# Feed-forward input by seven block products instead of eight, in three groups of two units

## The chip, the cores and the metric

The kernel runs on one core of a Trainium2 chip. The metric is the device time of one execution in microseconds (us), shorter being better. A core has five engines with a queue of instructions each: TensorE (PE, matmuls; its weight loads are shown apart as PEld), VectorE (DVE), ScalarE (ACT), GpSimd (POOL) and SyncE (SP, which here issues the transfers from memory). A difference of about 0.2% (1.25 us) is what a measurement of this kernel can tell from no change.

## What is computed

One layer of a decoder with 256 tokens and 1024 features: two mixers side by side, a cross-attention on 256 memory tokens, then a feed-forward block and a last normalisation. The change touches the feed-forward alone:

```python
hn = rmsnorm(h, norm_ffn_g[l])
gu = hn @ w_ffn_in[l]                       # 1024 -> 2 x 2816
h = h + (jax.nn.silu(gu[..., :FFN_HIDDEN]) * gu[..., FFN_HIDDEN:]) @ w_ffn_out[l]
return rmsnorm(h, final_norm_g)
```

Everything is float32. The kernel multiplies in a reduced format (`fp32r`) and keeps the precision by splitting every operand into a high and a low half and adding three products: high by high, high by low, low by high (`mm3t`, lines 237 to 240).

## The kernel before, in words

**Units.** All weights are read once, in units of 128 x 2048 numbers (1 MB), in the order that `plan` writes out (line 44). In the feed-forward, unit `("I", j, kh)` holds the rows `kh` (512 of 1024 features) of 256 gate columns and the matching 256 linear columns, laid side by side as 4 x 512 columns; unit `("O", j)` holds 256 rows of the output weights. There are 11 groups j: 22 input units and 11 output units, in the order I, I, O of the group before.

**Making a unit ready.** `prep` (line 169) lets SP fetch the unit into one of two `raw` buffers, ACT copies it into the high half (`hi`, line 194, two pieces of 1024 columns), and the low half `lo = raw - hi` (line 198) is shared: in each piece DVE takes 576 columns and POOL 448. There are three buffers each for `hi` and `lo`. `nxt` (line 205) makes units ready two ahead of the one in use.

**The cross-attention's output and the turn of h2.** The loop at line 1071 multiplies `wo` for two halves of tokens (t) and two halves of columns (c). `add_h` (line 915) adds the result to the residual H on DVE and sums its squares on ACT. `turn_h2` (line 1059) transposes one quarter of H on PE, DVE multiplies it by the norm's gain (`h2g`), ACT makes its high half `h2h` and POOL its low half `h2l`. Three quarters are turned inside that loop, the last one behind the first product of the feed-forward (line 1134). H is turned without the norm's factor; the factor (`rstd2`) comes in later, in `gate`, as a scale on each token.

**The feed-forward.** `ffn_in` (line 1104) adds one product into a PSUM bank `psi`: 128 tokens by 512 columns over 512 features, which is 4 x 3 matmuls of 512 columns. So a unit has two products (t = 0, 1), 24 matmuls. After the second unit of a group `gate` (line 1086) forms silu(gate) x linear with ACT and DVE. `turn_hid` (line 1094) transposes the 128 x 256 result on PE, ACT and DVE split it; it stands behind the next group's first unit. `ffn_out` (line 1119) multiplies with the output unit, 24 matmuls into four PSUM banks `acc` that are kept to the end.

**What sets the order.** The order on PE is that of the program (line 1252). On the other engines a planner places the instructions; a buffer with several users is waited for by semaphores. Each engine then takes its queue in order.

Of the kernel before, what the change touches and what calls it, by code (L numbers as in the profile page):

```python
# [10 lines left out]
F32 = mybir.dt.float32  # L11
F32R = mybir.dt.float32r
I32 = mybir.dt.int32
AF = mybir.ActivationFunctionType
# [53 lines left out]


ORDER = plan()  # L70


def lay(ws):
# [39 lines left out]
def bc(ap, n, axis):  # L113
    shape = list(ap.shape)
    shape.insert(axis, n)
    return ap.unsqueeze(axis).to_broadcast(shape)


def build(tc, A, out):
    nc = tc.nc  # L120
    V, SC, G, PE, SY = nc.vector, nc.scalar, nc.gpsimd, nc.tensor, nc.sync
    with ExitStack() as ctx:
# [28 lines left out]
        def bank(name, shape=(128, 512)):  # L151
            return sm.tile(list(shape), F32, name=name, tag="sm")
# [762 lines left out]
        def add_h(t, c, ps, scale, ssq):  # L915
            d = H[:, t, c * 512:(c + 1) * 512]
            if scale is None:
                V.tensor_tensor(d, ps, d, op=ALU.add)
            else:
                V.scalar_tensor_tensor(d, ps, scale, d, op0=ALU.mult, op1=ALU.add)  # L920
            j = t2b("hjunk")
            SC.activation(j, d, AF.Square, accum_out=ssq[:, t, c:c + 1])
# [129 lines left out]
        gfin = big("B4", "gfin", (128, 1024))  # L1052
        SY.dma_start(gfin, A["gfin"].to_broadcast([128, 1024]))
        H2 = big("P2", "H2", (128, 2, 8, 256), F32R)
        h2h, h2l = H2[:, 0], H2[:, 1]
        def wo_part(ps, t, c, kh):
            t_part(ps, wo[2 * c + kh], (oxh, oxl), t, kh)

        def turn_h2(t, c):
            ks, ts = slice(4 * c, 4 * c + 4), slice(t * 128, (t + 1) * 128)  # L1060
            bk = bank("h2T", (128, 4, 128))
            for j in range(4):
                k = 4 * c + j
                PE.transpose(bk[:, j], H[:, t, k * 128:(k + 1) * 128], ident)
            g = t2("h2g", (128, 4, 128))
            V.tensor_tensor(g, bk, bc(gv[:, V_FFN + 4 * c:V_FFN + 4 * c + 4], 128, 2), op=ALU.mult)
            SC.activation(h2h[:, ks, ts], g, AF.Copy)
            G.tensor_tensor(h2l[:, ks, ts], g, h2h[:, ks, ts].bitcast(F32), op=ALU.subtract)

        todo = None  # L1070
        for t in range(2):
            for c in range(2):
                ps = mm.tile([128, 512], F32, name="pso", tag="mm")
                wo_part(ps, t, c, 0)
                if todo:
                    turn_h2(*todo)
                wo_part(ps, t, c, 1)
                add_h(t, c, ps, None, ssq2)
                todo = (t, c)


        ring = ("B7", "B14", "B10", "B11", "B12", "B6")
        X2 = (h2h, h2l)
        hid, acc, two, psi, hm = {}, {}, {}, {}, {}

        def gate(o, t):
            r, ps = two["r"][:, t:t + 1], psi.pop((o, t))
            g = t2("fg", (128, 256))
            SC.activation(g, ps[:, 0:256], AF.Silu, scale=r)  # L1089
            u = t2b("fu", (128, 256))  # L1090
            V.scalar_tensor_tensor(u, ps[:, 256:512], r, g, op0=ALU.mult, op1=ALU.mult)  # L1091
            hm[o, t] = u

        def turn_hid(o):
            bk = mm.tile([128, 2, 256], F32, name="hidT", tag="mm")
            for t in range(2):
                u = hm.pop((o, t))
                for j in range(2):
                    PE.transpose(bk[:, j, t * 128:(t + 1) * 128], u[:, j * 128:(j + 1) * 128], ident)
            hd = big(ring[o % 6], "hid", (128, 2, 2, 256), F32R)  # L1100
            split(bk, hd[:, 0], hd[:, 1])
            hid[o] = hd

        def ffn_in(o, kh, t, w):
            if kh == 0:
                psi[o, t] = mm.tile([128, 512], F32, name="psi", tag="mm")
            t_part(psi[o, t], w, X2, t, kh)

        def out_part(o, w, t, c, home=None, u=0, v=512):
            if home is None and (t, c) not in acc:  # L1110
# [8 lines left out]
        def ffn_out(o):  # L1119
            w = by_k(nxt(), 2)  # L1120
            for t in range(2):
                for c in range(2):
                    out_part(o, w, t, c)

        for u in ORDER[at[0]:-2]:
            if u[0] == "O":
                ffn_out(u[1])
                continue
            _, o, kh = u
            w = by_k(nxt(), 4)  # L1130
            for t in range(2):
                ffn_in(o, kh, t, w)
                if (o, kh, t) == (0, 0, 0):
                    turn_h2(1, 1)
                    two["r"] = rstd2(ssq2, "h2")
                if kh == 1:
                    gate(o, t)
            if kh == 0 and o:
                turn_hid(o - 1)

        n = NF // 2 - 1
        wa = by_k(nxt(), 2)
        wb = by_k(nxt(), 2)
        out_part(n - 1, wa, 0, 0)
        turn_hid(n)
        out_part(n - 1, wa, 0, 1)
# [8 lines left out]


        ssq3 = cp.tile([128, 5], F32, name="ssq3")
        hg3 = {i: big(ring[j], "hg3", (128, 512)) for j, i in enumerate(((0, 0), (0, 1), (1, 0)))}  # L1160
# [95 lines left out]
```

## Time and profile before

| | us |
|---|---|
| median of 3 runs | 625.4 (624.79 to 625.51) |
| the profiled execution | 625.08 |
| its span (first to last instruction) | 623.1 |
| PE busy in the span | 615.1 |
| feed-forward, from its first matmul to its last | 431.12 to 616.63 |

The profile is one execution. Rows of the timeline give the start in us from the span's start, the duration in us, the engine, the line, the operation, `out<-in` by the program's names, the shape, and in brackets the idle time just before with what ended it. Rows of busy time in a stretch give PE, PEld, DVE, ACT and POOL in us (with the count of instructions), the granted PE clock as a share of full speed, the DMA share and GB/s. A PE record of a matmul covers its way through the array, so records of neighbours overlap. In groups, `xN` is the count; in the list of transfers the last number is the median time from issue to landing.

### The profile page before, as it was taken

What the parts mean: (1) busy time and instruction counts of PE and PEld (TensorE: products, weight loads), DVE (VectorE), ACT (ScalarE), POOL (GpSimd) and SP (SyncE); (2) the same over time, 40 slices, a digit from 0 to 9 for tenths busy, and PEclk for the clock granted to TensorE, in tenths of its full rate; (3) what the DMA queues carried; (4) which work ended last, traced back from release to release, by engine and by line L of the source; (5) the groups of instructions that cost most, each with busy time, mean ns of one, the idle gap of its engine ahead of it and who ended that gap; (6) DMA issues with size and microseconds to landing.
All of it is one profiled execution on the core that took longest, in us unless ns stands there. A gap on an engine that the chain in (4) does not pass through costs nothing.

```text
span 623.1 us, 8546 instructions
## 1 busy us (share of the span) xinstructions
PE 615.1 (99%) x3153; PEld 513.7 (82%) x3153; DVE 395.6 (63%) x691; ACT 334.1 (54%) x550; POOL 371.5 (60%) x296
## 2 busy tenths in 40 slices
PE   8999999999999999999999999999999999999995
PEld 7888888888877877778888888888888888888884
DVE  7589888979776875748846456754444444444433
ACT  7785554234376866727547556644543344434432
POOL 3888744556544564356857876656655665566553
PEclk9999999999999999999999999999999999999999
DMA  8754553334433333545454544453354455455511
GB/s 346 288 197 149 203 202 136 136 135 147 191 137 135 136 136 136 203 174 191 145 213 189 187 176 178 143 196 135 136 180 175 187 202 184 177 184 198 204 68 68
DMA packets 16890, 107.53 MB, mean 173 GB/s; under 512 B 2000, under 2 KB 2640, under 8 KB 4560
## 3 DMA queue, kind: packets, MB, share of 16 engines
q1 hardware_dynamic: 16128, 106.14, 46.9%
q10 hardware_dynamic: 720, 0.84, 0.4%
q8 instruction: 25, 0.41, 0.3%
q14 instruction: 17, 0.14, 0.1%
HBM read 105.92 MB, written 1.05 MB: 172 GB/s over the span
## 4 chain that ended last, share of the span: by engine, by line
PE 98%; DVE 0%; POOL 0%; issue 0%; POOLq 0%; DVEq 0%
PE pst L238 13%; PE pst L240 13%; PE pst L239 13%; PE psf L259 7%; PE psi L238 6%; PE psi L240 6%; PE psi L239 6%; PE psf L260 4%; PE acc L240 3%; PE acc L238 3%; PE acc L239 3%; PE lp L613 2%; PE psg L514 1%; PE pso L238 1%; PE pso L240 1%; PE pso L239 1%
## 5 line engine op out<-in xcount | busy, mean ns | idle before, releaser
L198 POOL TENSOR_TENSOR lo<-raw,hi 128x448 fp32r<-128x448 f32 x172 | 272.0, 1597 | 181.4 <-ACT hi L194 178.4
L194 ACT ACTIVATE hi<-raw 128x1024 fp32r<-128x1024 f32 (+1 forms) x194 | 196.2, 1037 | 161.1 <-PE pst L240 58.2
L198 DVE TENSOR_TENSOR lo<-raw,hi 128x576 fp32r<-128x576 f32 (+2 forms) x194 | 197.8, 1024 | 127.9 <-ACT hi L194 126.1
L238 PE MATMUL pst<-hi,XX 128*128 128x512 f32 x224 | 90.4, 404 | 0.0
L240 PE MATMUL pst<-hi,XX 128*128 128x512 f32 x224 | 87.4, 390 | 0.0
L239 PE MATMUL pst<-lo,XX 128*128 128x512 f32 x224 | 87.3, 390 | 0.0
L238 PE MATMUL psi<-hi,H 128*128 128x512 f32 x176 | 69.6, 395 | 0.0
L240 PE MATMUL psi<-hi,H 128*128 128x512 f32 x176 | 68.7, 390 | 0.0
L239 PE MATMUL psi<-lo,H 128*128 128x512 f32 x176 | 68.5, 389 | 0.0
L240 PEld LDWEIGHTS pst<-hi,XX 128*128 128x128 f32 x224 | 42.0, 188 | 9.0
L238 PEld LDWEIGHTS pst<-hi,XX 128*128 128x128 f32 x224 | 42.1, 188 | 8.8 <-issue 0.7
L239 PEld LDWEIGHTS pst<-lo,XX 128*128 128x128 f32 x224 | 42.1, 188 | 7.9
L240 PEld LDWEIGHTS psi<-hi,H 128*128 128x128 f32 x176 | 33.0, 188 | 7.1
L239 PEld LDWEIGHTS psi<-lo,H 128*128 128x128 f32 x176 | 33.1, 188 | 6.6
L238 PEld LDWEIGHTS psi<-hi,H 128*128 128x128 f32 x176 | 33.1, 188 | 6.5
L238 PE MATMUL acc<-hi,hid 128*128 128x512 f32 x86 | 33.6, 390 | 0.0
L240 PE MATMUL acc<-hi,hid 128*128 128x512 f32 x86 | 33.5, 389 | 0.0
L239 PE MATMUL acc<-lo,hid 128*128 128x512 f32 x86 | 33.5, 389 | 0.0
L1091 DVE SCALAR_TENSOR_TENSOR fu<-psi,r_h,fg 128x256 f32<-128x256 f32 x22 | 10.6, 483 | 25.1 <-ACT fg L1089 25.1
L1089 ACT ACTIVATE fg<-psi,r_h 128x256 f32<-128x256 f32 x22 | 10.4, 475 | 29.1 <-PE psi L240 29.1
L259 PE MATMUL psf<-H,hi 128*128 128x512 f32 x64 | 22.8, 400 | 0.0
L259 PE MATMUL psf<-XX,hi 128*128 128x512 f32 x64 | 22.6, 396 | 0.0
(336 smaller groups left out, 1199.4 us busy)
## 6 DMA issues: line engine op xcount, KB each, us to landing
raw<-w SPq DMA_DIRECT2D x94, 1024.0 KB, 4.8
raw<-w SPq DMA_DIRECT2D x4, 512.0 KB, 6.5
raw<-w SPq DMA_DIRECT2D x4, 256.0 KB, 4.0
H<-xtok SPq DMA_DIRECT2D x1, 1024.0 KB, 9.6
mraw<-mT SPq DMA_DIRECT2D x1, 1024.0 KB, 4.9
xraw<-xT SPq DMA_DIRECT2D x1, 512.0 KB, 6.5
gfin<-gfin SPq DMA_DIRECT2D x1, 512.0 KB, 3.7
out<-H SPq DMA_DIRECT2D x2, 256.0 KB, 2.0
```

The costliest lines, as they stand in the source:

```text
L194: SC.activation(hi[:, a], raw[:, a], AF.Copy)
L198: eng.tensor_tensor(lo[:, b], raw[:, b], hi[:, b].bitcast(F32), op=ALU.subtract)
L238: PE.matmul(ps, xh, h, start=first, stop=False)
L239: PE.matmul(ps, xh, l, start=False, stop=False)
L240: PE.matmul(ps, xl, h, start=False, stop=last)
L259: PE.matmul(ps, w[0][:, k, a], X2[:, :, k], start=k == 0, stop=False)
L260: PE.matmul(ps[:, 0], w[1][:, k, a], X2[:, 0, k], start=False, stop=k == 7)
L514: PE.matmul(pss[c][t], z[:, k, t * 128:(t + 1) * 128], ws[c][0][:, k], start=z is Xh and k == 0, stop=False)
L613: PE.matmul(ps[:, j], KS[:, a0 + j], QQ[:, a0 + j], start=True, stop=True)
L1089: SC.activation(g, ps[:, 0:256], AF.Silu, scale=r)
L1091: V.scalar_tensor_tensor(u, ps[:, 256:512], r, g, op0=ALU.mult, op1=ALU.mult)
```

## The change

The groups 2 and 3, 5 and 6, 8 and 9 are joined into three **double groups**. A double group has four input units: two halves of features by two groups. With the two halves of tokens this is a product of 2 x 2 by 2 x 2 blocks, which takes eight products of 12 matmuls. The change forms it from seven (P1 to P7), each a product of a sum of token blocks by a sum of weight blocks, with sums of the results. The groups 0, 1, 4, 7 and 10 stay as they were, with two products a unit.

- The list `FFN_PLAN` has 42 entries: 10 plain input units, 21 products, 11 output units. Its order is I0 I0 I1 I1, then P1 P2 O0 P6 P7 P5 O1 P3 P4 (entries 4 to 12), I4 I4 (13, 14), P1 P2 O2 P6 P7 O3 P5 O4 P3 P4 (15 to 24), I7 I7, P1 P2 O5 P6 P7 O6 P5 O7 P3 P4 (27 to 36), I10 I10, O8 O9 O10.
- The four chunks of a double group are fetched together (`load_blocks`, at the entries in `LOADS`) into four buffers of their own. DVE forms the sums of chunks in place (`both`, two pieces of 1024 columns): one at the load, one each ahead of P6, P5 and P4.
- Each of the 42 entries is split by `halve`: ACT in one piece of 2048 columns, DVE 1152 columns, POOL 896 (the first two entries still in two pieces). Every fourth entry uses a new buffer `px`, which lies where the cross-attention's output `ox` was, so four entries can be split at a time; they are prepared three ahead (`prep_u`).
- The sums of token blocks are made once (`token_sums`): four additions on DVE, four pairs of high and low half on ACT and POOL.
- Products are added up in PSUM where they can be; three times a double group ACT copies a partial sum away (`keep`) and DVE adds it to another bank (`whole`).
- The norm's factor is now applied to H ahead of the turn (`rstd_h2`). The first tokens are turned in the last part of the `wo` loop; then the first four units are multiplied for the first tokens, then the second tokens are turned, then the same four units are multiplied for the second tokens.
- The inner units are turned at the entries in `TURNS`, later than before relative to their gate.

```diff
+SEVEN = ("P1", "P2", "P6", "P7", "P5", "P3", "P4")
...
+LOADS = {0: (2,), 10: (5,), 22: (8,)}
+TURNS = {4: (0,), 8: (1,), 15: (2,), 18: (3,), 20: (4,), 27: (5,), 30: (6,), 32: (7,), 38: (8, 9)}
...
+        px = big("P1", "px", (128, 4096), F32R)
...
+        def halve(raw, n):
+            if n % 4 == 3:
+                hi, lo = px[:, 0:2048], px[:, 2048:4096]
+            else:
+                hi = wh.tile([128, 2048], F32R, name="hi", tag="hi")
+                lo = wl.tile([128, 2048], F32R, name="lo", tag="lo")
+            pieces = 2 if n < 2 else 1
+            w = 2048 // pieces
+            for c in range(pieces):
+                a = slice(c * w, (c + 1) * w)
+                SC.activation(hi[:, a], raw[:, a], AF.Copy)
+                cut = (c + 1) * w - POOL_COLS // pieces
+                V.tensor_tensor(lo[:, c * w:cut], raw[:, c * w:cut], hi[:, c * w:cut].bitcast(F32), op=ALU.subtract)
+                G.tensor_tensor(lo[:, cut:a.stop], raw[:, cut:a.stop], hi[:, cut:a.stop].bitcast(F32),
+                                op=ALU.subtract)
+            return hi, lo
...
+        def both(out, x, y, op):
+            for i in range(2):
+                a = slice(1024 * i, 1024 * i + 1024)
+                V.tensor_tensor(out[:, a], x[:, a], y[:, a], op=op)
+
+        def load_blocks(q):
+            blk.clear()
+            for key, tag, c in (("22", "B12", (q + 1, 1)), ("12", "B6", (q + 1, 0)),
+                                ("11", "B10", (q, 0)), ("21", "B11", (q, 1))):
+                blk[key] = big(tag, "b" + key, (128, 2048))
+                SY.dma_start(blk[key], A["w"][where[("I",) + c]])
...
+                both(blk["12"], blk["22"], blk["12"], ALU.subtract)
+
+        def block(name):
+            if name == "P6":
+                both(blk["11"], blk["12"], blk["11"], ALU.add)
+            elif name == "P5":
+                both(blk["12"], blk["22"], blk["11"], ALU.subtract)
+            elif name == "P4":
+                both(blk["21"], blk["21"], blk["11"], ALU.subtract)
+            return blk[{"P1": "11", "P2": "21", "P6": "11", "P7": "12", "P5": "12", "P3": "22", "P4": "21"}[name]]
...
+        def rstd_h2(t):
+            V.tensor_scalar(v2[:, t:t + 1], ssq2[:, 2 * t:2 * t + 1], ssq2[:, 2 * t + 1:2 * t + 2], EPS,
+                            op0=ALU.add, op1=ALU.add)
+            G.tensor_tensor(r2[:, t:t + 1], v2[:, t:t + 1], nhalf[:, :1], op=ALU.pow)
+            hn = []
+            for c in range(2):
+                n = t2("hn")
+                SC.activation(n, H[:, t, c * 512:(c + 1) * 512], AF.Copy, scale=r2[:, t:t + 1])
+                hn.append(n)
+            return hn
...
+        def keep(key, ps, home):
+            SC.activation(home, ps, AF.Copy)
+            kept[key] = home
+
+        def whole(q, t, ps, key):
+            c = t2("fc")
+            V.tensor_tensor(c, ps, kept.pop(key), op=ALU.add)
+            psi[q, t] = c
+            gate(q, t)
+
+        def ffn_product(n):
+            _, q, name = units[n]
+            w = by_k(pair[n], 4)
+            key = {"P1": "A", "P6": "A", "P5": "A", "P3": "A", "P2": "B", "P7": "F", "P4": "F"}[name]
...
+            product(ps, name, w, first)
+            if name == "P1":
+                keep("1", ps, t2("f1"))
+            elif name == "P2":
+                whole(q, 0, ps, "1")
+            elif name == "P6":
+                keep("2", ps, gf[:, 1024:1536])
+            elif name == "P5":
+                keep("4", ps, gf[:, 1536:2048])
+                whole(q + 1, 1, bank_of["F"], "4")
+            elif name == "P3":
+                psi[q + 1, 0] = ps
+                gate(q + 1, 0)
+            elif name == "P4":
+                whole(q, 1, ps, "2")
...
+        prep_u(3)
+        for n in range(4):
+            ffn_in(n, 0)
+        turn_h2(1, hn1)
+        for n in range(4):
+            for q in LOADS.get(n, ()):
+                load_blocks(q)
+            ffn_in(n, 1)
+            if n == 0:
+                token_sums()
+            prep_u(n + 4)
+        for n in range(4, len(units) - 2):
+            for q in LOADS.get(n, ()):
+                load_blocks(q)
+            prep_u(n + 3)
+            for o in TURNS.get(n, ()):
+                turn_hid(o)
...
```

More of the change, by code (lines that the diff above doesn't have):

```diff
@@ L1055, in build @@
         h2h, h2l = H2[:, 0], H2[:, 1]
+        where = {u: i for i, u in enumerate(ORDER)}
+        px = big("P1", "px", (128, 4096), F32R)
+        made_u, pair, blk = [0], {}, {}
+        def halve(raw, n):
[14 more added lines that the diff above has]
+            return hi, lo
@@ new lines, in block, with prep_u @@
+        def block(name):
[6 more added lines that the diff above has]
+            return blk[{"P1": "11", "P2": "21", "P6": "11", "P7": "12", "P5": "12", "P3": "22", "P4": "21"}[name]]
+        units = FFN_PLAN
+        def prep_u(upto):
+            while made_u[0] <= min(upto, len(units) - 1):
+                n = made_u[0]
+                made_u[0] += 1
+                u = units[n]
+                if u[0] == "P":
+                    raw = block(u[2])
+                else:
+                    raw = wr.tile([128, 2048], F32, name="raw", tag="raw")
+                    SY.dma_start(raw, A["w"][where[u]])
+                pair[n] = halve(raw, n)
@@ new lines, in tokens, with product @@
+        def tokens(name):
+            if name in ("P1", "P2", "P4"):
+                t, kh = {"P1": (0, 0), "P2": (0, 1), "P4": (1, 1)}[name]
+                return [[z[:, 4 * kh + k, t * 128:(t + 1) * 128] for k in range(4)] for z in X2]
+            i = {"P5": 0, "P6": 1, "P7": 2, "P3": 3}[name]
+            return [[SS[:, z, i, k] for k in range(4)] for z in range(2)]
+        def product(ps, name, w, first):
+            xh, xl = tokens(name)
+            for k in range(4):
+                for i, (x, z) in enumerate(((xh, w[0]), (xh, w[1]), (xl, w[0]))):
+                    PE.matmul(ps, x[k], z[:, k], start=first and k == 0 and i == 0, stop=k == 3 and i == 2,
+                              skip_group_check=not first)
@@ L1121, in ffn_out @@
+        def ffn_out(n):
+            w = by_k(pair[n], 2)
             for t in range(2):
                 for c in range(2):
[L1123 to L1139, printed above, removed]
+                    out_part(units[n][1], w, t, c)
@@ L1143, in build @@
         n = NF // 2 - 1
-        wa = by_k(nxt(), 2)
-        wb = by_k(nxt(), 2)
+        wa, wb = (by_k(pair[len(units) - 2 + i], 2) for i in range(2))
         out_part(n - 1, wa, 0, 0)
```

130 lines of the change are left out of this document (96 added, 34 removed).

## The prediction

> **What bounds the kernel now.** I read the page's busy times first, then the chain that ended last, then the busy times of the feed-forward stretch alone.
>
> ```profile
> span 623.1 us, 8546 instructions
> ...
> PE 615.1 (99%) x3153; PEld 513.7 (82%) x3153; DVE 395.6 (63%) x691; ACT 334.1 (54%) x550; POOL 371.5 (60%) x296
> ```
> ```profile
> PE 98%; DVE 0%; POOL 0%; issue 0%; POOLq 0%; DVEq 0%
> ```
> ```profile
> 431.12:616.63 185.51, 185.51 (x847) 153.59 (x845) 83.43 (x103) 80.29 (x105) 107.80 (x68) 1.00 0.45 165
> ```
>
> The last row (PE, PEld, DVE, ACT, POOL, clock, DMA share, GB/s) is the feed-forward: 33 units in 185.51 us, PE without a gap, at full clock. DVE is busy 45% of it, POOL 58%. So PE alone sets the end, and anything that leaves its stream shortens the kernel, as long as the weights stay ahead of it. Steps between matmuls:
>
> ```profile
> 440.00 0.39 PE L239 MATMUL psi<-lo,H 128*128 128x512 f32 x1
> ...
> 445.21 0.39 PE L238 MATMUL psi<-hi,H 128*128 128x512 f32 x1
> ```
> ```profile
> 448.10 0.44 PE hidT L1099 x4
> 464.89 0.44 PE hidT L1099 x4
> ```
>
> Between the first two rows lie 23 steps in 5.21 us: a matmul costs 0.2265 us, not the 0.39 of its record, which overlaps its neighbours. Twelve of them (one product) cost 2.72 us, a unit of 24 costs 5.44. The second pair is one round of three units: 16.79 us, of which 72 matmuls take 16.31, so turning one inner unit (four transposes) costs 0.47.
>
> Next I looked at who may not work at the same time. These are DVE and POOL around 328 us, and the same DVE line (L926, two columns wide) while POOL was idle:
>
> ```profile
> 328.92 1.12 DVE L926 TENSOR_TENSOR s<-ssq 128x2 f32<-128x2 f32 x1
> ...
> 432.86 0.16 DVE L926 TENSOR_TENSOR s<-ssq 128x2 f32<-128x2 f32 x1 [0.85 <-ACT hjunk L922]
> ```
> ```profile
> 328.29 1.74 POOL L198 TENSOR_TENSOR lo<-raw,hi 128x448 fp32r<-128x448 f32 x1 [3.35 <-ACT hi L194]
> ...
> 330.99 1.15 POOL L198 TENSOR_TENSOR lo<-raw,hi 128x448 fp32r<-128x448 f32 x1
> ```
>
> A two-column subtraction that takes 0.16 us alone took 1.12 and ended at 330.04, just when POOL's instruction ended (330.03). POOL's half split takes 1.15 us when DVE leaves it alone and 1.74 when DVE's split began 0.05 us earlier. So a DVE instruction with two SBUF inputs and a POOL instruction take turns, each for its whole length; I call what they share **the pair**. A DVE instruction that reads PSUM is not held up: the next row ran in its usual 0.68 us inside POOL's busy time from 449.38 to 452.70.
>
> ```profile
> 449.95 0.68 DVE L286 TENSOR_TENSOR hid<-hidT,hid 128x512 fp32r<-128x512 f32 x1
> ```
> ```profile
> 449.38 3.32 POOL L198 TENSOR_TENSOR lo<-raw,hi 128x448 fp32r<-128x448 f32 x2 [1.83 <-ACT hi L194]
> ```
>
> The Trainium skill, "SBUF — State Buffer", section "SBUF: two separate sides", says the same: a DVE instruction with two SBUF inputs and a GpSimd instruction exclude each other for the whole instruction. It speaks against this change, since the two busy shares (45% and 58%) then add up. Without that rule the sum would be rival A below, with it it is the forecast.
>
> One weight split now:
>
> ```profile
> 460.62 0.76 DVE L198 TENSOR_TENSOR lo<-raw,hi 128x576 fp32r<-128x576 f32 x1 [2.74 <-ACT hi L194]
> 461.57 1.44 DVE L198 TENSOR_TENSOR lo<-raw,hi 128x576 fp32r<-128x576 f32 x1 [0.19 <-ACT hi L194]
> ```
> ```profile
> 460.67 3.35 POOL L198 TENSOR_TENSOR lo<-raw,hi 128x448 fp32r<-128x448 f32 x2 [1.77 <-ACT hi L194]
> ```
>
> From 460.62 to 464.02 the pair is never free: 3.40 us of every 5.44. That fits. A product of 2.72 us with a split of its own does not.
>
> **The change, part by part.** *Fewer matmuls.* Each double group multiplies seven blocks where eight stood: 3 x 2.72 = **8.16 us** less PE, 36 matmuls. Transposes stay in number.
>
> *More splits and sums.* Seven products need seven splits where four units needed four: 42 splits in place of 33. Prices:
>
> ```profile
> 332.75 0.41 DVE L251 TENSOR_TENSOR kx<-psf,ku 128x256 f32<-128x256 f32 x1
> ...
> 434.48 0.69 DVE L1066 TENSOR_TENSOR h2g<-h2T,gv 128x512 f32<-128x512 f32 x1 [1.25 <-PE h2T L1064]
> ```
> ```profile
> 333.69 0.74 POOL L973 TENSOR_TENSOR kxl<-kx,kxh 128x256 fp32r<-128x256 f32 x1 [1.55 <-ACT kxh L972]
> ...
> 435.92 1.29 POOL L1068 TENSOR_TENSOR H<-h2g,H 128x512 fp32r<-128x512 f32 x1 [1.91 <-ACT H L1067]
> ```
>
> DVE costs 1.09 ns a column and 0.13 us a start ((0.69-0.41)/256), POOL 2.15 ns and 0.19. A split in one piece saves a start of each: 3.40-0.13-0.19 = 3.08 at the least, 3.40 at the most; I take 3.2. A sum of two chunks (2 x 1024 columns, two SBUF inputs) is 2 x (0.13+1.12) = 2.5, less the overlap of ends, at the least 2.2 (the columns alone); I take 2.3. The gate of a product summed in SBUF holds the pair 0.4 (the 256-column row), 0.3 at the least. The token sums are 4 DVE of 0.7 and 4 POOL of 1.3.
>
> *The pair's account* runs from T, the end of the first tokens' pass over four units (431.12 + 4 x 2.72 = 442.0), to the split of the last product, P4 of the third group, unit 36. It holds 33 splits x 3.2 = 105.6; 11 sums x 2.3 = 25.3 (three a group, and one at two of the fetches; the first fetch's falls before T); 9 gates x 0.4 = 3.6; two low parts of the late tokens 2.6; token sums 8.0: **145.1 us**. It starts at T + 2.1, since the late turn's first POOL step came that long after its transposes:
>
> ```profile
> 433.85 0.60 PE L1064 MATMUL h2T<-cst,H 128*128 128x128 f32 x4
> ```
>
> *PE's account* for the same stretch, to the start of that product: 8 transposes 0.9, second pass 10.9, 20 products 54.4, 8 output units and 4 input units 65.3, eight turns 3.8: **135.3 us**. So PE waits at least 2.1 + 145.1 - 135.3 = 11.9 us, and the kernel loses 11.9 - 8.2 = 3.7 even if the pair never rests. Four pairs of split buffers (the new one in the place of `ox`) let the pair run at most four units ahead, so an early surplus can't be saved up.
>
> *The pair's rest.* A sum must be followed by ACT's high half before its split can begin:
>
> ```profile
> 459.53 2.01 ACT L194 ACTIVATE hi<-raw 128x1024 fp32r<-128x1024 f32 x2 [3.12 <-PE acc L240]
> ```
>
> For 2.0 us the pair has nothing of that unit; whether another fills it hangs on the queues of DVE and POOL, which are taken in order. At the least it happens once (P5 directly behind P7 in the first group: its sum overwrites the chunk that P7's split still reads), 2 us; at the most at all nine, 18. No row decides, I take the middle, **10 us**. Behind a waiting DVE stand the inner unit's low half and the sums of kept products, so some of PE's waits will name `hidT` or `whole`'s line.
>
> *The late turn.* h2 of the second tokens is turned directly ahead of its use. By the rows at 433.85 and 435.92 its low half ends 3.36 us after the first transpose; PE has 0.9 of transposes and 0.45 of matmuls in between: 2.0 us of wait, already inside the account from T. The scaling that moved ahead of it (a power, two scaled copies) has the 10.9 us of the first pass as cover; without that cover it would cost its own 2 us.
>
> *Covered.* Keeping a product on ACT costs about 0.6 and has a product or an output unit (2.72 or more) before its bank is written again; without that cover, 0.6 each, nine times. ACT: 42 x 2.0 plus some 30 of small work, out of 180. Bytes are the same.
>
> *Sum:* -8.2 + 11.9 + 10 = **+13.7**; the profiled execution's 625.08 (span 623.1 and 2.0 around it; the median of runs is 625.4) becomes 638.8, **639**. By the low prices (3.08, 2.2, 0.3) and no rest at all: 139.1 in the pair, 5.9 of wait, 622.8. By the high prices (3.40, 2.5) and all rests: 153.9, 20.7 + 18 of wait, 655.6.
>
> **The rivals.** *A, faster: the pair keeps up.* If DVE's and POOL's work lies beside each other after all, each has room (83.43 and 107.80 of 185.51), and only the late turn's 2.0 remains: 625.1 - 8.2 + 2.0 = **619**. The turning point is a split that holds the pair 2.84 us: (135.3 - 2.1 - 39.5)/33. The 3.40 and the 1.12 us rows speak against it. Chance 0.15. *Just even*, with the pair full and prices low, 624 to 626: 0.05.
>
> *B, the fetches come late.*
>
> ```profile
> raw<-w SPq DMA_DIRECT2D x94, 1024.0 KB, 4.8
> ```
>
> The loads at units 10 and 22 put four chunks into SP's queue ahead of the next plain unit's weights; the last chunk may be fetched only when P4's split has read it. If SP keeps that order, the plain unit is ready 4.8 + 4.8 + 2.0 + 3.2 = 14.8 us after that split, while PE has P4's 2.72 left: 12 us, twice, whatever the pair does: 625.1 - 8.2 + 2 + 24 = **643**. Its raw buffer is free long before, so SP can issue it earlier: 0.10.
>
> *C, the clock falls in the waits.*
>
> ```profile
> 600.00:623.00 23.00, 16.63 (x81) 13.78 (x79) 9.42 (x18) 7.84 (x18) 8.36 (x7) 0.96 0.13 47
> ```
>
> The only row below full clock has 6.4 us of idle PE: 0.04 x 23 = 0.9 us of clock lost. If one wait in each group is long enough and the product behind it (2.72) then runs at half rate, that adds 3 x 2.72 = 8.2 to the forecast: **647**. The Trainium skill, "TensorE: Matmul & The Clock Gate", section "HAM oscillation — how this bites in real kernels", puts the bound at gaps of about 3.4 us; no wait in this trace tests it. 0.08.
>
> **How the numbers follow.** Forecast (pair-bound, 626 to 655) 0.58, B 0.10, C 0.08, worse than 655 0.04, A 0.15, even 0.05. Range 623 to 655: it leaves out A and the worst, 0.19. A difference of 0.2% (1.25 us) is about what a measurement can tell: faster 0.15, same 0.05, slower 0.80.
>
> **What would show it.** 36 matmuls fewer. PE gaps in the feed-forward of some 22 us, ended by `lo` (DVE or POOL), mostly ahead of P6, P5 and P4 and the plain units behind them; POOL's single split of 896 columns near 2.1 us alone and over 3 beside a DVE sum; the sums' 1024 columns at 1.2 us alone. If gaps are only about 2 us, the pair kept up (A). If `raw` DMAs end the gaps, it is B; if the granted clock is well below 1 there, C. Wrong would be above all the rest of 10 us, and the order in which the queues are taken.

## The result, and the profile after

The changed kernel takes 647.39 us (median, 645.91 to 648.66) beside 625.31 us (624.79 to 625.51) of the kernel before on the same chip: 1.0354 times as long, 95% interval 1.0327 to 1.038. The forecast was 639 us, with a range of 623 to 655. The profiled execution of the changed kernel took 646.6 us.

First the page's head, the shares of the chain that ended last, and the list of transfers. Line numbers are those of the changed kernel: `halve` is L1098 (ACT), L1100 (DVE) and L1101 (POOL), the sums of weight chunks are L1109, a gate's product L1206, a product's matmuls L1267, those of the plain and output units L263 to L265, and an inner unit's low half L311.

```profile
span 644.5 us, 8470 instructions
...
PE 616.0 (96%) x3117; PEld 511.3 (79%) x3117; DVE 464.8 (72%) x706; ACT 354.9 (55%) x545; POOL 394.8 (61%) x279
...
PE 78%; DVE 8%; issue 5%; POOL 4%; ACT 3%; DMA 2%; POOLq 0%; DVEq 0%; ACTq 0%
...
raw<-w SPq DMA_DIRECT2D x82, 1024.0 KB, 4.8
b<-w SPq DMA_DIRECT2D x12, 1024.0 KB, 4.8
```

PE has 3117 matmuls in place of 3153: the 36 that the change removes are gone. But PE's share of the chain fell from 98% to 78%, and DVE and POOL have 12% of it. Transfers land as fast as before, and the chain holds 2% of them. In the feed-forward one sum waited for a fetched chunk (2.2 us, up to 547.83), while splits held the pair.

The feed-forward as one stretch (the columns are PE, PEld, DVE, ACT, POOL, granted clock, DMA share, GB/s), and what PE waited for in the whole kernel:

```profile
430.00:617.00 187.00, 166.59 (x716) 134.79 (x715) 146.63 (x107) 94.42 (x87) 123.42 (x47) 0.94 0.43 161
```
```profile
PE acc L265 <- DVE hids L311: 9.1, 1, 9.1
PE pqB L1267 <- DVE fu L1206: 8.1, 2, 4.5
PE psi L263 <- ACT H L1178: 2.0, 1, 2.0
...
PE psi L265 <- POOL H L1179: 0.8, 2, 0.5
PE pqB L1267 <- POOL lo L1101: 0.3, 1, 0.3
```

PE is idle for 187.00 - 166.59 = 20.4 us there, where it had no gap before, and the list accounts for all of it (20.3). DVE was busy 45% of its stretch and is now busy 78%, POOL 66% after 58%; the two together pass 100% (an instruction that is held up counts as busy). The clock is 0.94 instead of 1.00. No line names a transfer. The waits are few and long: one of 9.1 us, two of 4.5 and 3.6, one of 2.0.

What DVE and POOL did during the longest one, 464.7 to 473.8, ahead of output unit 0:

```profile
464.25 5.78 DVE L1109 TENSOR_TENSOR b<-b,b 128x1024 f32<-128x1024 f32 x2
469.96 3.22 DVE L1100 TENSOR_TENSOR px<-b,px 128x1152 fp32r<-128x1152 f32 x1
473.10 0.68 DVE L311 TENSOR_TENSOR hids<-hidT,hids 128x512 fp32r<-128x512 f32 x1
473.70 1.34 DVE L1100 TENSOR_TENSOR lo<-b,hi 128x1152 fp32r<-128x1152 f32 x1
```
```profile
462.75 3.20 POOL L1101 TENSOR_TENSOR lo<-raw,hi 128x896 fp32r<-128x896 f32 x1
465.91 3.04 POOL L1101 TENSOR_TENSOR px<-b,px 128x896 fp32r<-128x896 f32 x1
468.92 3.05 POOL L1101 TENSOR_TENSOR lo<-b,hi 128x896 fp32r<-128x896 f32 x1
```

PE waits for the 0.68 us instruction at 473.10. It reads PSUM and doesn't need the pair, but it stands in DVE's queue behind two pieces of a sum and a split, and each of these is held up by one of POOL's. The split took 3.22 us at 469.96 beside POOL, and its like 1.34 at 473.70 after POOL had ended.

### The profile page after: what moved, and what is told of

Its sections match the earlier page's. It is cut to its first block, busy times and chain, and to the rows that moved or that the text cites. A ratio compares the mean times of both kernels' runs of the same rounds, so it can differ in the third digit from the quotient of the medians.

```text
span 644.5 us, 8470 instructions
## 1 busy us (share of the span) xinstructions
PE 616.0 (96%) x3117; PEld 511.3 (79%) x3117; DVE 464.8 (72%) x706; ACT 354.9 (55%) x545; POOL 394.8 (61%) x279
## 4 chain that ended last, share of the span: by engine, by line
PE 78%; DVE 8%; issue 5%; POOL 4%; ACT 3%; DMA 2%; POOLq 0%; DVEq 0%; ACTq 0%
PE pst L263 13%; PE pst L265 12%; PE pst L264 12%; PE psf L284 7%; PE psf L285 3%; DVE b L1109 3%; DVE lo L1100 2%; PE pqA L1267 2%; PE acc L265 2%; PE acc L263 2%; PE acc L264 2%; POOL lo L1101 2%; ACT hi L1098 2%; PE lp L638 2%; POOL px L1101 1%
## 5 line engine op out<-in xcount | busy, mean ns | idle before, releaser
L223 POOL TENSOR_TENSOR lo<-raw,hi 128x448 fp32r<-128x448 f32 x106 | 161.7, 1540 | 110.6 <-ACT hi L219 107.6
L219 ACT ACTIVATE hi<-raw 128x1024 fp32r<-128x1024 f32 (+1 forms) x128 | 128.8, 1028 | 94.5 <-PE pst L265 56.0
L223 DVE TENSOR_TENSOR lo<-raw,hi 128x576 fp32r<-128x576 f32 (+2 forms) x128 | 129.8, 1021 | 58.8 <-ACT hi L219 57.8
L263 PE MATMUL pst<-hi,XX 128*128 128x512 f32 x224 | 90.4, 404 | 0.0
L265 PE MATMUL pst<-hi,XX 128*128 128x512 f32 x224 | 87.4, 390 | 0.0
L1101 POOL TENSOR_TENSOR lo<-raw,hi 128x896 fp32r<-128x896 f32 (+1 forms) x21 | 56.5, 2695 | 29.0 <-ACT hi L1098 29.0
L1101 POOL TENSOR_TENSOR lo<-b,hi 128x896 fp32r<-128x896 f32 x13 | 40.0, 3076 | 25.7 <-ACT hi L1098 22.4
L1098 ACT ACTIVATE hi<-raw 128x2048 fp32r<-128x2048 f32 (+1 forms) x21 | 36.6, 1751 | 27.3 <-issue 18.0
L1100 DVE TENSOR_TENSOR lo<-raw,hi 128x1152 fp32r<-128x1152 f32 (+1 forms) x21 | 38.2, 1825 | 15.7 <-ACT hi L1098 15.6
L265 PEld LDWEIGHTS pst<-hi,XX 128*128 128x128 f32 x224 | 42.1, 188 | 9.0
L263 PEld LDWEIGHTS pst<-hi,XX 128*128 128x128 f32 x224 | 42.1, 188 | 8.8 <-issue 0.7
L1109 DVE TENSOR_TENSOR b<-b,b 128x1024 f32<-128x1024 f32 x24 | 42.8, 1808 | 2.2 <-DMA b<-w 2.2
L265 PE MATMUL acc<-hi,hids 128*128 128x512 f32 x78 | 31.5, 404 | 9.1 <-DVE hids L311 9.1
L1098 ACT ACTIVATE hi<-b 128x2048 fp32r<-128x2048 f32 x13 | 24.9, 1917 | 22.4 <-DVE b L1109 13.6
L263 PE MATMUL acc<-hi,hids 128*128 128x512 f32 x78 | 31.6, 405 | 0.0
L263 PE MATMUL psi<-hi,H 128*128 128x512 f32 x72 | 28.7, 399 | 2.0 <-ACT H L1178 2.0
L1100 DVE TENSOR_TENSOR lo<-b,hi 128x1152 fp32r<-128x1152 f32 x13 | 21.9, 1682 | 11.8 <-ACT hi L1098 11.8
L265 PE MATMUL psi<-hi,H 128*128 128x512 f32 x72 | 28.8, 400 | 0.8 <-POOL H L1179 0.8
L264 PE MATMUL psi<-lo,H 128*128 128x512 f32 x72 | 28.5, 396 | 0.0
```

The lines of the kernel that those rows point to most:

```text
L219: SC.activation(hi[:, a], raw[:, a], AF.Copy)
L223: eng.tensor_tensor(lo[:, b], raw[:, b], hi[:, b].bitcast(F32), op=ALU.subtract)
L263: PE.matmul(ps, xh, h, start=first, stop=False)
L264: PE.matmul(ps, xh, l, start=False, stop=False)
L265: PE.matmul(ps, xl, h, start=False, stop=last)
L1098: SC.activation(hi[:, a], raw[:, a], AF.Copy)
```

## The experiments

All but one start from the changed kernel. Times are medians with their spread, ratios are against the kernel before with their 95% interval.

**One. The subtraction on DVE alone.** POOL's columns go to DVE.

```diff
-                cut = (c + 1) * w - POOL_COLS // pieces
-                V.tensor_tensor(lo[:, c * w:cut], raw[:, c * w:cut], hi[:, c * w:cut].bitcast(F32), op=ALU.subtract)
-                G.tensor_tensor(lo[:, cut:a.stop], raw[:, cut:a.stop], hi[:, cut:a.stop].bitcast(F32),
-                                op=ALU.subtract)
+                V.tensor_tensor(lo[:, a], raw[:, a], hi[:, a].bitcast(F32), op=ALU.subtract)
```

> The changed kernel, but every split in the feed-forward is made by DVE alone (2048 columns), POOL's share is gone. Theory (the pair of DVE and POOL is the bound, POOL's columns cost it twice what DVE's cost): a split holds the pair 0.13 + 2048 x 1.09 ns = 2.36 us in place of 3.2, so the account from the first pass to the last product falls from 145 to 117 us of 135 of PE; the late turn's 2 us and 2 to 6 of order effects stay: 619 to 627 us, granted clock 0.99 or more in the feed-forward. Rival (DVE itself is overloaded, its queue is the bound): it gets 33 x 896 columns, some 32 us, more work: 665 us or more. Rival B (fetches late): no change, 645 to 650.

Measured: 627.24 us (626.71 to 627.58), ratio 1.0029 (1.0018 to 1.004), at the upper edge of the 619 to 627 expected. The feed-forward stretch, a window of it on DVE, and PE's waits:

```profile
430.00:620.00 190.00, 180.97 (x820) 147.80 (x818) 148.25 (x124) 103.34 (x105) 18.99 (x13) 1.00 0.44 164
```
```profile
506.66 1.22 DVE L1106 TENSOR_TENSOR b<-b,b 128x1024 f32<-128x1024 f32 x1
507.79 2.29 DVE L1099 TENSOR_TENSOR lo<-b,hi 128x2048 fp32r<-128x2048 f32 x1
```
```profile
PE acc L265 <- DVE hids L311: 2.8, 2, 1.8
...
PE pqA L1264 <- DVE lo L1099: 1.4, 1, 1.4
PE psi L263 <- ACT H L1175: 1.4, 1, 1.4
```

Taking the second engine away makes the kernel 20 us faster. DVE's busy time barely grows (148.25 us in 190), because before it spent much of it standing still beside POOL. A whole split takes 2.29 us on DVE alone; shared with POOL one ended every 3.0 to 3.2 us (POOL's 3.20, 3.04 and 3.05 rows above). So the forecast's mechanism holds: the two exclude each other, and an overloaded DVE and the late fetch both fall. The clock is 1.00, and no wait of the feed-forward passes 1.8 us.

**Two. No sums of weight chunks.**

```diff
         def both(out, x, y, op):
-            for i in range(2):
-                a = slice(1024 * i, 1024 * i + 1024)
-                V.tensor_tensor(out[:, a], x[:, a], y[:, a], op=op)
+            return
```

> The changed kernel without the twelve sums of weight chunks: the products multiply the chunks as they were fetched, the rest of the computation and all splits stay, so its output is not the reference's. Theory (pair): the account falls by 25 us to 120 us beside 135 of PE, which leaves the late turn's 2 us and 2 to 6 us of order effects: 619 to 627 us, clock near 1. If the splits alone were enough to stop PE, 635 us or more. Rival B (fetches late): the fetches are the same, 643 to 650.

Measured: 623.33 us (622.37 to 625.05), ratio 0.9971 (0.9961 to 0.9981).

```profile
430.00:620.00 190.00, 180.87 (x816) 148.32 (x815) 118.01 (x101) 103.02 (x104) 142.14 (x53) 0.98 0.46 168
```

Without the sums the pair keeps up though POOL still splits, and with the same fetches. Together with PE's waits in the changed kernel, none of which names a transfer, this puts the late fetch (rival B) out. By the forecast's own account it should: 2.1 + 145.1 - 25.3 is 121.9 us beside PE's 135.3.

**Three. The sums on POOL instead of DVE.**

```diff
-                V.tensor_tensor(out[:, a], x[:, a], y[:, a], op=op)
+                G.tensor_tensor(out[:, a], x[:, a], y[:, a], op=op)
```

> The changed kernel with the twelve sums of weight chunks on POOL in place of DVE. Theory (pair): a sum of two pieces costs POOL 2 x (0.19 + 1024 x 2.15 ns) = 4.8 us against 2.3, eleven sums add 27 us to the account, all of it wait of PE, with some clock lost: 672 to 685 us. Rival (DVE is overloaded, POOL has room): DVE loses 25 us of work, 630 us or less.

Measured: 662.59 us (661.54 to 663.63), ratio 1.0595 (1.0572 to 1.0617). The direction is that of the theory, the size is below its band: 15 us more than the changed kernel where 25 or more were expected.

```profile
430.00:620.00 190.00, 160.40 (x658) 127.53 (x657) 110.92 (x78) 88.25 (x83) 180.62 (x69) 0.90 0.40 148
```

POOL is now busy 95% of the stretch. Moving work to the engine with the lower share makes it slower, since POOL does a column in twice DVE's time while DVE stands still. The trace shows why it is 15 us and not 27: from the second tokens' turn (442.88) to the end of the last P4's split (617.64) the rows of POOL and of DVE's work with SBUF inputs, laid over each other, take the pair for 171.7 of 174.8 us. In the changed kernel it is 145.2 of 159.5. So the work grew by 26.5, as expected, but the rests fell from 14.3 to 3.0, and 15.3 us are left. The expectation had kept the rests as they were.

**Four. All splits in two pieces.** If the long holds were what hurts, shorter ones would help.

```diff
-            pieces = 2 if n < 2 else 1
+            pieces = 2
```

> The changed kernel with every split in two pieces (1024 columns on ACT, 576 on DVE, 448 on POOL), as the kernel before has them. Theory (pair): each split costs two more starts, 0.2 to 0.3 us, 33 times, 7 to 10 us more in the account, partly paid back since the DVE instructions that read PSUM wait behind shorter ones: 645 to 657 us. Rival (not the sum of work but the long single holds of 2 to 3 us are the cause): clearly faster, 640 us or less.

Measured: 651.15 us (648.76 to 653.55), ratio 1.0412 (1.0366 to 1.0453). No gain in either of its two executions: the length of one hold is not the cause.

**Five. DVE alone, and the second tokens turned one unit earlier.** The edit of the first experiment, and:

```diff
         for n in range(4):
+            if n == 3:
+                turn_h2(1, hn1)
             ffn_in(n, 0)
-        turn_h2(1, hn1)
```

> The changed kernel with DVE alone at the splits, as in the run before, and the second tokens turned one product earlier, ahead of the first tokens' product with unit 3. Theory (the late turn's wait is a chain of 3.4 us that nothing covers): with a product of 2.72 us behind the transposes the wait falls from 2.0 us to at most 0.3, and about as much of the waits of the first double group may go with it: 624 to 625.5 us against 627.2 without. Rival (the waits of the first group come from DVE's queue alone, which the earlier turn doesn't shorten): the 2 us return at the first products of the double group, 626.5 to 627.5.

Measured: 626.2 us (625.8 to 627.01), ratio 1.0024 (1.0013 to 1.0034), about 1 us less than the first experiment, between the two expectations; against the kernel before, the two intervals overlap. The waits at the turn (1.4 and 0.6) are gone, and PE's listed waits in the feed-forward fall from 7.6 to 4.5 us in all. But behind one of them, in the first double group, the clock falls, which it did nowhere in the first experiment's feed-forward:

```profile
474.41 0.49 PE L1264 MATMUL pqA<-hi,SS 128*128 128x512 f32 x1 [0.65 <-ACT hi L1098]
476.74 0.80 PE L1264 MATMUL pqA<-lo,SS 128*128 128x512 f32 x1 [1.83 <-DVE lo L1099]
...
482.86 0.40 PE L263 MATMUL acc<-hi,hids 128*128 128x512 f32 x1
```

From 476.74 to 482.86 lie 14 steps, which would take 3.2 us at 0.2265 and took 6.1: the clock took back most of what the waits gave.

**Six. And the plain units between the double groups.** The edit of the fifth, with another order; `LOADS` and `TURNS` follow it.

```diff
-    out = two(0) + two(1)
-    out += seven(2, P2=[0], P5=[1]) + two(4)
-    out += seven(5, P2=[2], P7=[3], P5=[4]) + two(7)
-    out += seven(8, P2=[5], P7=[6], P5=[7])
-    out += two(10) + [("O", 8)]
+    out = two(0) + two(1) + two(4)
+    out += seven(2, P2=[0], P5=[1]) + two(7)
+    out += seven(5, P2=[2], P7=[3], P5=[4]) + two(10)
+    out += seven(8, P2=[5], P7=[6])
+    out += [("O", 7), ("O", 8)]
```

> The kernel of the earlier turn with each plain pair of input units moved one place ahead: group 4 before the first double group, 7 before the second, 10 before the third, and output unit 7 behind the last product. Theory (only the first double group still waits, since token sums, the sum at the fetch and the first splits come at once; 10.9 us more of PE work ahead of it let DVE catch up): all but 1 or 2 us of the saving of 8.2 us is kept, 617.5 to 620 us, faster than both kernels. Rival (a double group alone keeps DVE busier than PE, wherever it stands): the waits move to the later groups, 623 to 627.

Measured: 624.37 us (623.53 to 625.01), ratio 0.999 (0.9981 to 0.9999). The expected 617.5 to 620 was missed by more than 4 us.

```profile
PE acc L265 <- DVE hids L311: 2.1, 3, 1.7
...
PE psi L264 <- DVE lo L1099: 0.9, 1, 0.9
PE psi L265 <- POOL H L1176: 0.3, 1, 0.3
```
```profile
597.01 0.40 PE L264 MATMUL acc<-px,hids 128*128 128x512 f32 x1
599.06 0.50 PE L265 MATMUL acc<-px,hids 128*128 128x512 f32 x1 [1.65 <-DVE hids L311]
599.40 0.40 PE L263 MATMUL acc<-px,hids 128*128 128x512 f32 x1
```

The first product's waits of the fifth experiment went, but 3.8 us stay (two more waits are 0.3 and 0.2), the most of it ahead of output unit 8. The feed-forward takes 183.9 us (431.85 to 615.79), 6.6 more than 185.5 - 8.16. The 2.8 us beyond the listed waits lie mostly around them. The steps at 597.01 and 599.06 take 2.05 and 0.34 us, together 0.29 more than two steps of 0.2265 and the listed 1.65. There are eight such places, one of them with a wait too short for the list: about 2 us. The stretch also holds four transposes more than in the kernel before, by estimate 0.5 us (0.47 for four).

**Seven. The kernel before with the feed-forward's subtraction on DVE alone.** This tells whether DVE alone is better everywhere.

```diff
-                cut = (c + 1) * n - (0 if i in ALONE else POOL_COLS // pieces)
+                cut = (c + 1) * n - (0 if i in ALONE or ORDER[i][0] in "IO" else POOL_COLS // pieces)
```

> The kernel before, with the feed-forward's splits made by DVE alone and nothing else changed. Theory (the pair is no bound there: 3.4 us of every 5.44): no difference, 624.5 to 626 us. Rival (splits by DVE alone are better everywhere, and the run with seven products gained from that, not from the pair): faster by 2 us or more.

Measured: 625.45 us (624.92 to 626.15), ratio 1.0009 (0.9999 to 1.0018). No difference that the measurement can tell: where the pair has room, the sharing costs nothing.

**Eight. Extra matmuls in a wait, at the wrong place.** Is the lower clock a loss of its own? 28 extra matmuls were to fill the long wait.

```diff
             else:
+                if n == 10:
+                    idle = mm.tile([128, 512], F32, name="idle", tag="mm")
+                    for i in range(28):
+                        PE.matmul(idle, h2h[:, 0, 0:128], h2h[:, 0:2], start=True, stop=True)
                 ffn_out(n)
```

> The changed kernel with 28 matmuls added whose result nobody reads, 6.3 us of PE work, placed where PE waits 9.1 us, ahead of output unit 1. Theory (a wait of over 3.4 us or so halves the clock and the next dozen matmuls cost 0.43 us in place of 0.23): the matmuls fit into the wait, less than 3 us of idle time is left, the slow matmuls behind it are gone, 2 to 2.5 us off that stretch: 644.5 to 646 us. Rival (the slow steps have another cause, such as the operands): the same 647.4, with the slow steps in their place. If the added work doesn't fit, 650 or more.

Measured: 651.06 us (649.77 to 652.07), ratio 1.0419 (1.0405 to 1.0433). A miss: the long wait stands at output unit 0 (entry 6), not at unit 1 (entry 10), and it is as long as before. It says one thing all the same: 28 x 0.2265 = 6.3 us of added PE work cost 3.7, and PE's wait for `fu` fell from 8.1 to 5.1:

```profile
PE acc L265 <- DVE hids L311: 9.4, 2, 9.1
PE pqB L1267 <- DVE fu L1206: 5.1, 2, 4.4
```

**Nine. The same at the right place.** `if n == 6` instead of `if n == 10`.

> The changed kernel with 28 extra matmuls ahead of output unit 0 (their result is used by nothing, all of the layer is still computed). They have half the columns' worth of nothing to wait for, so PE works through most of the 9.1 us wait that stands there in the changed kernel. Clock theory: the wait itself still ends when the low half of the inner units is ready, about 473.8 us, but the clock does not fall and the dozen matmuls behind it keep their 0.23 us step instead of 0.43: some 2.4 us less than the changed kernel, 644.5 to 645.5. Rival (the 0.43 us steps come from the operands of that unit, not from the idle time): steps unchanged, 647 to 648. If the extra matmuls outlast the wait: above 648.

Measured: 648.36 us (645.99 to 649.27), ratio 1.0359 (1.0337 to 1.038): no gain, where 644.5 to 645.5 were expected. Yet the clock did what the theory said. The 12 us behind that wait, in the changed kernel and then in this one:

```profile
473.00:485.00 12.00, 11.17 (x41) 9.03 (x42) 7.96 (x9) 4.96 (x5) 4.67 (x2) 0.75 0.28 93
```
```profile
474.00:486.00 12.00, 10.91 (x50) 9.00 (x51) 9.51 (x9) 6.83 (x6) 4.42 (x2) 1.00 0.30 95
```

The clock column rises from 0.75 to 1.00: fed matmuls, PE keeps it. But the time was given back at later waits. The changed kernel, then this one:

```profile
519.64 0.53 PE L1267 MATMUL pqB<-hi,H 128*128 128x512 f32 x1 [4.51 <-DVE fu L1206]
```
```profile
475.08 0.50 PE L265 MATMUL acc<-hi,hids 128*128 128x512 f32 x1 [2.46 <-DVE hids L311]
...
507.36 0.50 PE L264 MATMUL psi<-lo,H 128*128 128x512 f32 x1 [1.02 <-DVE lo L1100]
...
521.12 0.79 PE L1267 MATMUL pqB<-hi,H 128*128 128x512 f32 x1 [5.03 <-DVE fu L1206]
```

From the end of the first wait to the end of the second lie 45.81 us in the changed kernel (473.83 to 519.64) and 46.04 here (475.08 to 521.12). So between these two waits the clock doesn't set the time; the pair does.

**Ten. Extra matmuls in the last wait.** Behind the last wait nothing can take the gain back. The matmuls add zero to an output bank.

```diff
+        nil = cp.tile([128, 128], F32R, name="nil")
+        SC.activation(nil, ident, AF.Copy, scale=0.0)
...
             elif u[0] == "P":
+                if n == 28:
+                    for i in range(15):
+                        PE.matmul(acc[0, 0], nil, h2h[:, 0:2], start=False, stop=False, skip_group_check=True)
                 ffn_product(n)
```

> The changed kernel with 15 extra matmuls (3.4 us) directly ahead of P2 of the third double group, where PE waits 3.56 us in the changed kernel, the last wait of its feed-forward. They add zero times the tokens to an output bank, so nothing is left out. Theory (half clock is given back by the pair's next wait, as the filled first wait showed, so only the slow matmuls behind the last wait count in the end): the dozen 0.43 us steps behind it go, no wait follows that could take the gain, 2.0 to 2.5 us less: 644.5 to 645.5. Rival (no slow step counts, something later still sets the end): 647 to 648. Rival (every slow step had counted, and the first filled wait failed for another reason): cannot be told from the theory here.

Measured: 644.94 us (644.66 to 645.4), ratio 1.0319 (1.0305 to 1.0333), 2.45 us less than the changed kernel, as expected. The two intervals just overlap, since the changed kernel's executions spread from 645.91 to 648.66; the executions themselves don't. The 10 us from that wait's end, in the changed kernel and then here:

```profile
572.00:582.00 10.00, 9.21 (x30) 7.42 (x31) 8.71 (x9) 2.22 (x2) 4.06 (x2) 0.70 0.32 105
```
```profile
572.00:582.00 10.00, 9.88 (x43) 7.51 (x42) 9.97 (x8) 2.37 (x2) 5.46 (x2) 1.00 0.28 107
```

Ten to twelve matmuls at 0.43 instead of 0.23 us are 2.0 to 2.5 us. The rows agree: P2's twelve took 5.26 us in the changed kernel (572.79 to 578.05) and 2.85 here (573.59 to 576.44), 2.4 less.

**Eleven. The sixth with the last turns earlier.**

```diff
-TURNS = {..., 39: (8, 9)}
+TURNS = {..., 38: (9,)}
...
                 for c in range(2):
+                    if (n, t, c) == (38, 1, 1):
+                        turn_hid(8)
                     out_part(units[n][1], w, t, c)
```

> The kernel with the subtractions on DVE alone and the plain units between the double groups, and the last inner units turned earlier: group 9 ahead of output unit 7, group 8 ahead of the last quarter of output unit 7 (before: both ahead of output unit 8, where PE waited 1.65 and 0.25 us). Theory (that wait is the path): 1.5 to 2 us less than 624.4, 622.4 to 623, so 0.35 to 0.45% faster than the kernel before. Rival (the wait is for DVE's queue and moves with the turn): 624 to 625.

Measured: 624.09 us (623.1 to 625.53), ratio 0.9982 (0.9973 to 0.9991), 0.3 us less than the sixth, which the measurement can't tell from none. The rival holds: the wait is still 1.71 us, for the low half of unit 8, which stands in DVE's queue behind another split.

```profile
595.41 2.29 DVE L1099 TENSOR_TENSOR lo<-raw,hi 128x2048 fp32r<-128x2048 f32 x1 [0.59 <-ACT hi L1098]
597.62 0.68 DVE L311 TENSOR_TENSOR hids<-hidT,hids 128x512 fp32r<-128x512 f32 x1
```

Of the versions tried that compute the whole layer it is the fastest. Its interval lies just below 1, by less than the 0.2% that counts here.

**Twelve. One sum later in DVE's queue.** P4's sum of the third double group, which stood ahead of the gates that P2 waits for, is written where it can't run early.

```diff
+                if late:
+                    both(blk["12"], blk["21"], blk["11"], ALU.subtract)
+                    return blk["12"]
                 both(blk["21"], blk["21"], blk["11"], ALU.subtract)
...
-                    raw = block(u[2])
+                    raw = block(u[2], u[1] == 8)
```

> The changed kernel with one sum of the third double group later in DVE's queue: P4's sum of weight chunks is written over P5's chunk, so it can't run before P5's chunk is split. In the changed kernel its two pieces stand in DVE's queue directly ahead of the split and the two gates for which P2 of that group waits 3.56 us, 33 us before P4 is multiplied. Nothing else moves in the queues, nothing is left out. Theory (there the order of DVE's queue sets the end, and the pair is ahead again by P4): the wait falls by the two pieces' 2.4 us to 1.1, too short for the half clock behind it, whose 2.45 us go as well: 642 to 643. Rival (the pair has no room to spare, the sum costs the same later): a wait of about 2.4 us at P4 or the outputs ahead of it takes the place, 645 with the clock kept, 647 if it falls there.

Measured: 649.37 us (647.83 to 650.25), ratio 1.0388 (1.0372 to 1.0405); its interval overlaps that of the changed kernel. The theory falls. The rival holds in kind, though the time is above its 645 to 647. P2 of that group no longer waits, but output unit 7 does:

```profile
598.46 0.73 PE L265 MATMUL acc<-hi,hids 128*128 128x512 f32 x1 [3.27 <-DVE hids L311]
598.99 0.63 PE L263 MATMUL acc<-hi,hids 128*128 128x512 f32 x1
```
```profile
585.81 5.61 DVE L1109 TENSOR_TENSOR b<-b,b 128x1024 f32<-128x1024 f32 x2
...
594.57 3.24 DVE L1100 TENSOR_TENSOR px<-b,px 128x1152 fp32r<-128x1152 f32 x1
597.73 0.68 DVE L311 TENSOR_TENSOR hids<-hidT,hids 128x512 fp32r<-128x512 f32 x1
```

The moved sum takes 5.61 us beside POOL's splits, stands with two splits ahead of an inner unit's low half, and the clock falls behind the new wait too (a step of 0.53 to 598.99, then of 0.43).

## Why the prediction was right, and where it was wrong

**The mechanism** is shown: the first three experiments move work off the pair (-20 us), take work out (-24) and put more on (+15), and the time follows each time. PE's listed waits, 20.3 us, also lie near the forecast's 21.9 (11.9 + 10), but this is partly luck, since the kernel lost 22 us and not 13.7. The difference stands in slow steps behind the waits: 8.4 us above 0.2265 a step, in four places (1.7, 2.5, 1.7 and 2.5). What lies ahead of another wait fills time in which PE would have waited otherwise (shown for the first long wait by the ninth experiment).

**The saving** of 8.16 us is there (36 matmuls), but only a kernel whose pair keeps up can show it.

**The pair's account** was forecast as 2.1 us of start, 145.1 of work and 10 of rest from T to the end of P4's split: 157.2. The rows that bound it in the changed kernel:

```profile
441.41 1.03 PE L1175 MATMUL h2T<-cst,hn 128*128 128x128 f32 x8
```
```profile
587.13 1.36 DVE L1100 TENSOR_TENSOR lo<-b,hi 128x1152 fp32r<-128x1152 f32 x1 [2.04 <-ACT hi L1098]
```
```profile
597.60 3.32 POOL L1101 TENSOR_TENSOR lo<-b,hi 128x896 fp32r<-128x896 f32 x1 [0.71 <-ACT hi L1098]
```
```profile
606.23 0.39 PE L1267 MATMUL pqF<-hi,H 128*128 128x512 f32 x1
```

It ran from 441.41 to 600.92: 159.5 us. Laying all rows of POOL and of DVE's work with SBUF inputs over each other, the pair was taken for 145.2 us of it and free for 14.3, of which the late turn's start is 1.7; three of its rests are the 2.0 us of ACT after a sum (the row at 587.13 is one). So start and rest, 12.1 in the forecast, measured 14.3: 2.3 us too little in all. That the rest of 10 came so near is partly luck: it was the middle of 2 to 18, and of the 12.6 us measured only the three ACT rests, 6.1, are of the kind that the forecast named. The other 6.5 are gaps of 0.2 to 1.4 us (and two under 0.1), mostly while DVE ran an instruction that reads PSUM and POOL had nothing ready; the forecast had no term for them. The price of a split (3.2) is what the alternating rows show, and a sum's 2 x 1.21 in the changed kernel's single rows is close to the 2.3 taken. The late turn's wait was forecast as 2.0 and listed as 2.0.

**The step that failed** is the next one, that PE's account ends where the pair's does. P4 is multiplied at 606.23, 5.3 us after its split. PE's last wait stands 33 us earlier:

```profile
572.79 0.80 PE L1267 MATMUL pqB<-hi,H 128*128 128x512 f32 x1 [3.56 <-DVE fu L1206]
```

From there the pair needs 28.1 us to 600.92, while PE has 30.9 us of its own work at 0.2265 a step (P2, P6, P7, P5, P3, units 5, 6 and 7, two turns), and the half clock behind the wait adds 2.5. The pair had work in hand for later products while PE stood for a gate. So the balance is: forecast 638.8; +2.3 for the account, +2.8 for the work that PE still had when the pair was ahead, +2.5 for the clock = 646.4, beside 646.6 of the profiled execution. The three terms are read from that execution up to the start of P4, so only the last 0.2 us, for all that lies behind it, are a check on the sum.

**The place of the waits** was wrong with it. They were to stand ahead of P6, P5 and P4, ended by `lo`. They stand at output unit 0 and at P2 of the second and third group, ended by `hids` and `fu`: instructions that don't need the pair, behind ones that do, in a queue that is taken in order. The prediction named that possibility and the queue order as a doubt, but priced no more than the total. The twelfth experiment shows that it isn't one badly placed sum: moved, the wait comes back elsewhere. Whether an order of DVE's queue would save the 2.8 us stays open.

**Rival C** gave 647 us, the measured number, for another reason. Its behaviour is there: behind waits of 9.1, 4.5 and 3.6 us the steps are 0.43 us (clock 0.75 and 0.70 in the windows shown, 0.72 from 519.00 to 525.00); the Trainium skill, "TensorE: Matmul & The Clock Gate", section "HAM oscillation — how this bites in real kernels", puts the bound at gaps of about 3.4 us, and these three waits agree (shorter ones are shown below that don't). But it adds its 2.5 us only once, behind the last wait (tenth experiment); ahead of that it fills time in which PE would have waited (ninth). Adding 3 x 2.72 to a time that the pair sets was wrong. **Rivals A and B** are out by the waits listed and by the second experiment. The cover of `keep` on ACT held: no wait names it.

## What to carry to other kernels

Before a change takes matmuls from a PE that is 99% busy, add up what the other engines must do per matmul afterwards, and add engines that exclude each other as one. If such a pair becomes the bound, give the work to its faster engine alone before anything else: here that brought back 20 of 22 us. While such a pair sets the time, a loss of PE ahead of another of its waits (here the lower clock) is not added to the sum; only what stands behind the last wait is.

## What the runs showed of the hardware

A subtraction shared by DVE (1152 columns) and POOL (896) was slower than DVE alone: 3.2 us against 2.29, since both take turns and POOL's columns cost twice as much. POOL's 896 columns took 2.17 us alone (569.01 in the changed kernel) and up to 3.32 where DVE's instruction came first:

```profile
569.01 2.17 POOL L1101 TENSOR_TENSOR lo<-b,hi 128x896 fp32r<-128x896 f32 x1 [3.12 <-PE pqA L1267]
```

The half clock came behind waits shorter than that bound of the Trainium skill: 3.27 us at output unit 7 in the twelfth experiment, 1.83 us in the fifth (with 0.65 one step earlier), and in the changed kernel the late turn's 2.0 us, followed by one of 0.5, has four steps of 0.43 us behind it:

```profile
446.41 0.63 PE L263 MATMUL psi<-hi,H 128*128 128x512 f32 x1
446.83 0.63 PE L264 MATMUL psi<-lo,H 128*128 128x512 f32 x1
```

So at least three waits here differ from the Trainium skill, and the measurement decides. Nor does the length of one wait decide alone: 2.46 us in the ninth experiment (475.08) and 1.76 in the first had no slow step behind them. What does decide stays open. Matmuls whose result nothing uses, 15 and 28 of them, filled all or most of such a wait and kept the clock at 1.00 in the two windows shown.
